# Adding the second part of half of the feed-forward weights by DMA, and three more pairs with seven block products

## The chip, the cores and the metric

The kernel runs on one core of one Trainium2 chip. The metric is device microseconds (us) of one execution. The median of three runs before the change is 1647.92 us (1647.09 to 1648.18).

## The reference, cut to what matters

A trunk of two layers works on 256 latent and 256 context tokens of width 1024. Each layer is a SwiGLU feed-forward block (FFN), a token mixer, and a second FFN:

```
D_MODEL = 1024; SEQ = CTX_LEN = 256; DEPTH = 2; D_FF = 2816

def swiglu(h, w_i, w_o):
    g, u = jnp.split(h @ w_i, 2, axis=-1)
    return (jax.nn.silu(g) * u) @ w_o

def trunk_layer(...):
    xl = xl + 0.5 * g1l * swiglu(modulate(rmsnorm(xl, norm_w[0]), sh1l, sc1l), w_ffn1_in, w_ffn1_out)
    xc = xc + 0.5 * g1c * swiglu(modulate(rmsnorm(xc, norm_w[0]), sh1c, sc1c), w_ffn1_in, w_ffn1_out)
    ...                      # the mixer: latent attention and a short convolution, then w_out
    xl = xl + 0.5 * g3l * swiglu(modulate(rmsnorm(xl, norm_w[2]), sh3l, sc3l), w_ffn2_in, w_ffn2_out)
    if not last:
        xc = ...             # the same for the context
```

Shifts, scales and gates come from `silu(c) @ w_ada[i] + b_ada[i]`. In the second layer the context stops after the mixer, so the last FFN has 256 tokens; the three FFNs before it have 512.

## The kernel before, in words

**Two parts of each number.** TensorE multiplies in its `float32r` type. Each operand is kept as two such tiles: the high part is the number cast to `float32r` (`whi`, `h`, `hid`), and the low part is the number minus the high part (`wlo` for weights). A product is three matmuls (`mm3`, L227 to L229): high by high, high by low, low by high. `split` makes the parts: ScalarE casts (L233), VectorE subtracts (L234).

**Weights.** `wload` (L206) loads a weight tile of 128x1024 (512 KB) into one of three `wraw` buffers by a DMA that SP issues, and splits it into one of five `whi` and one of five `wlo` buffers. Such a tile holds eight blocks of 128x128. Inside the mixer every fourth tile has its subtraction on GpSimd (L221).

**FFN, first product.** The 2816 hidden columns are 22 pairs of a gate block and an up block of 128 columns, 11 pairs in each of two halves. `gated` computes a pair plainly: two weight tiles, 2x8 blocks, three matmuls of 512 tokens each, 48 matmuls. `gated_fast` computes a pair with seven products of half-size matrices in place of eight (Winograd's form): 7 x 4 blocks x 3 matmuls of 256 tokens, 84 matmuls. It needs sums of weight blocks, made in place in `wraw` by four VectorE operations (L454 to L458), four split tiles (`wg`, `w22` of half size, `s12`, `s34`), and more VectorE operations on the results (L485 to L495). `FAST` lists the pairs done so: 6, 8 and 8 of 22 in the three FFNs of 512 tokens. The last FFN (`ffn_end`) has none.

**FFN, second product.** After each half, `into_x` multiplies 11 tiles of the output weights (`f1o`, `f2o`) with the hidden blocks: eight output blocks, each a sum of 11 blocks by three matmuls of 512 tokens, and adds them to X (L346). In the second half, the last three output blocks are done for the context first and then for the latents (`apart`), and the norm of the next part starts between them: squares on ScalarE, sums on VectorE and TensorE, a power -1/2 on GpSimd (`r`, L248), its broadcast on TensorE (`psn_r`, L251), then `t` (L301), `h` (L302) and the low part of `h` (L303).

**Modulation.** `ada` puts loads of `w_ada` (512 KB each) and two VectorE operations for each between the other work, at a rate set by `PACE`.

**Order.** The kernel is written in program order, and a scheduler arranges each engine's instructions by a model of time when it is built; `issue_after` holds some behind others. Each engine then works its own list in order. A DMA that waits holds whatever stands behind it on the engine that issues it: SP for the loads, GpSimd for the DMAs of the change.

Of the kernel before, what the change touches and what calls it, by code (L numbers as in the profile page):

```python
# [13 lines left out]
AF = mybir.ActivationFunctionType  # L14
ALU = mybir.AluOpType
# [5 lines left out]
NKT = D // P  # L21
# [18 lines left out]
WCH = 1024  # L40
# [15 lines left out]
LEAD = 1  # L56
EARLY_AT = (1, 1, 2, 2, 3, 3)
NT1 = 3
PACE = ((0.9, 2.15), (0.8, 1.7), (0.9, 1.75))
FAST = ((8, 10, 13, 15, 17, 19), (6, 8, 10, 12, 14, 16, 18, 20), (6, 8, 10, 12, 14, 16, 18, 20))  # L60


@with_exitstack
def tile_kernel(ctx: ExitStack, tc: tile.TileContext, xT, ctxT, cT, cR, w_ada, b_ada, norm_w,
                f1i, f1o, f2i, f2o, f2r, w_in, qn_w, kvn_w, w_uq, w_ukv, conv_w, w_out, fin_w,
                qtab, out):
    nc = tc.nc
# [137 lines left out]

    turn, pooled = [0], [False]  # L206

    def wload(src, n, tags=("whi", "wlo"), by=None):
        raw = slot("wraw", "wraw")[:, :n]
        load(raw, src)  # L210
        if by is not None:
            nc.vector.tensor_tensor(raw, raw, by, ALU.mult)
        w = [slot(t, "w" + p, dtype=F32R)[:, :n] for t, p in zip(tags, ("hi", "lo"))]
        turn[0] += 1
        if not (pooled[0] and turn[0] % POOLED == 0):
            split(*w, raw)
            return w
        nc.scalar.copy(w[0], raw)  # L218
        for a in range(0, n, TT):
            c = slice(a, a + TT)  # L220
            nc.gpsimd.tensor_tensor(w[1][:, c], raw[:, c], f32(w[0][:, c]), ALU.subtract)  # L221
        return w
# [9 lines left out]
    def split(hi, lo, src, eng=nc.vector):  # L232
        nc.scalar.copy(hi, src)  # L233
        return eng.tensor_tensor(lo, src, f32(hi), ALU.subtract)  # L234
# [19 lines left out]
    class Norm:  # L254
# [38 lines left out]
        def apply(self, s, R, kt):  # L293
# [5 lines left out]
            hi, lo = (h[:, cs] for h in self.H[kt])  # L299
            t1 = small.tile([P, T], F32, tag="t1", name="t1", bufs=NT1)  # L300
            nc.vector.scalar_tensor_tensor(t1, x, mod(d, 3 * i + 1, s, kt), R, ALU.mult, ALU.mult)  # L301
# [18 lines left out]
    def into_x(d, gate, streams, src, xs, nxt, pace=(0, 0)):  # L320


        n = len(xs)
        held = {}
        if nxt is not None and nxt.d < DEPTH and len(streams) == 1:
            ada_until(nxt.d, 3 * nxt.i + 1)

        def block(b):
            i = b // NKT
            if i not in held:  # L330
                held[i] = wload(src(i), WCH)
            return [v[:, b % NKT * P:(b % NKT + 1) * P] for v in held[i]]

        for ms in (range(0, NKT - SKEW), range(NKT - SKEW, NKT)):
            apart = nxt is not None and ms.stop == NKT
            if apart and nxt.d < DEPTH:
                ada_until(nxt.d, 3 * nxt.i + 1)
            for c in spans(streams, apart):
                for m in ms:
                    pt = mmtile(c)  # L340
                    for k in range(n):
                        mm3(pt, block(m * n + k), [v[:, c[0]:c[1]] for v in xs[k]], k == 0, k == n - 1)
                    for s in streams:
                        if c[0] <= s * T < c[1]:
                            xm = X[m][:, s * T:(s + 1) * T]
                            end = nc.vector.scalar_tensor_tensor(xm, pt[:, s * T - c[0]:(s + 1) * T - c[0]],  # L346
                                                                 mod(d, gate, s, m), xm, ALU.mult, ALU.add)
                            if nxt is not None:
                                nxt.add(m, s)
                                if nxt.d < DEPTH and len(streams) == 1:  # L350
                                    nxt.ahead(m, s)
                    if not apart:
                        ada(pace[1], end)
                if apart:
                    nxt.finish(c[0] // T)


    def gated(d, wi, j, nrm, streams):
# [1 line left out]
        H = nrm.H  # L360
        done = [early.pop(0) for _ in range(2)] if early else None
        if not done:
            w = [wload(wi[d, j, gu], WCH) for gu in range(2)]
        hid = pair(HID[j % HALF % 3], "hid")
        if nrm.AX and j < NAHEAD:

# [24 lines left out]
    def moving_sums(H):  # L391
# [44 lines left out]
            put(3, x)  # L436
        return out

    def gated_fast(d, wi, j, H, sums):

        g, u = (slot("wraw", "wraw") for _ in range(2))
        load(g, wi[d, j, 0])
        load(u, wi[d, j, 1])
        a, b = slice(0, TT), slice(TT, WCH)

        def parts(src):
            n = src.shape[-1]
            w = [slot(t, "w" + p, dtype=F32R)[:, :n] for t, p in (("whi", "hi"), ("wlo", "lo"))]
            split(*w, src)
            return w  # L450

        wg = parts(g)
        w22 = parts(u[:, b])
        nc.vector.tensor_tensor(g[:, a], g[:, a], u[:, a], ALU.subtract)  # L454
        nc.vector.tensor_tensor(u[:, a], u[:, a], u[:, b], ALU.add)
        nc.vector.tensor_tensor(u[:, b], u[:, b], g[:, a], ALU.subtract)
# [144 lines left out]
    def mixer(d, H, last, nxt):  # L601
# [15 lines left out]
        for c in spans([0, 1], True):  # L617
# [6 lines left out]
            product(ps, w[1], H, c)  # L624
            k1 = small.tile([P, T], F32, tag="t1", name="k1", bufs=NT1)
            k2 = small.tile([P, T], F32, tag="t1", name="k2", bufs=NT1)
            nc.vector.scalar_tensor_tensor(k1[64:96], ps[96:128], math.sqrt(QKD), qtb[96:128, cs], ALU.mult, ALU.mult)
# [145 lines left out]
        def attend(h, s, pT):  # L773
# [9 lines left out]
            r = slice(h % 2 * VD, (h % 2 + 1) * VD)  # L783
            o = small.tile([P, T], F32, tag="t1", name="o1", bufs=NT1)[r]
            nc.scalar.copy(o, ps[VD:P])
# [178 lines left out]
```

## Time and profile before

| | |
|---|---|
| median of three runs | 1647.92 us |
| the profiled execution | 1648.4 us, span 1646.6 us |
| TensorE (PE) busy | 1612.0 us, 98% |
| VectorE (DVE) busy | 1248.0 us, 76% |
| ScalarE (ACT) busy | 688.4 us, 42% |
| GpSimd (POOL) busy | 57.6 us, 3% |
| loads from SP's queue | 247.62 MB, 44.1% of 16 DMA engines |

The profile is of one execution. "Busy" is time in which an engine executed something; the DMA share is the mean over the core's 16 DMA engines. A row of a group gives line, engine, operation, output and inputs, shapes, count, then busy time and the mean of one in ns, then the idle time just before and who ended it. A row of the timeline gives start, duration, engine, line, operation, tile, shape and count. A matmul's recorded duration is its way through the array; the next one starts before it is over.

### The profile page before, as it was taken

What the parts mean: (1) busy time and instruction counts of PE and PEld (TensorE: products, weight loads), DVE (VectorE), ACT (ScalarE), POOL (GpSimd) and SP (SyncE); (2) the same over time, 40 slices, a digit from 0 to 9 for tenths busy, and PEclk for the clock granted to TensorE, in tenths of its full rate; (3) what the DMA queues carried; (4) which work ended last, traced back from release to release, by engine and by line L of the source; (5) the groups of instructions that cost most, each with busy time, mean ns of one, the idle gap of its engine ahead of it and who ended that gap; (6) DMA issues with size and microseconds to landing.
All of it is one profiled execution on the core that took longest, in us unless ns stands there. A gap on an engine that the chain in (4) does not pass through costs nothing.

```text
span 1646.6 us, 24595 instructions
## 1 busy us (share of the span) xinstructions
PE 1612.0 (98%) x9677; PEld 1415.4 (86%) x9677; DVE 1248.0 (76%) x2071; ACT 688.4 (42%) x1103; POOL 57.6 (3%) x65
## 2 busy tenths in 40 slices
PE   6999999999999999999999999999999999999998
PEld 5889889889877788988998888988998998989997
DVE  5597898888477578879887879876776578776665
ACT  4434224424476443431343243431443257754443
POOL 0000000001211000000000000000000011100000
PEclk9999999999999999999999999999999999999999
DMA  9434664562222124346444533365346333345553
GB/s 374 144 114 155 223 197 162 175 205 103 72 80 71 52 103 141 122 160 211 160 140 168 192 111 116 133 233 190 128 147 219 103 99 114 128 156 190 182 190 105
DMA packets 73364, 249.72 MB, mean 152 GB/s; under 512 B 8736, under 2 KB 12960, under 8 KB 73248
## 3 DMA queue, kind: packets, MB, share of 16 engines
q1 hardware_dynamic: 72960, 247.62, 44.1%
q8 instruction: 76, 1.25, 0.3%
q10 hardware_dynamic: 288, 0.52, 0.1%
q14 instruction: 40, 0.33, 0.1%
HBM read 246.28 MB, written 1.05 MB: 150 GB/s over the span
## 4 chain that ended last, share of the span: by engine, by line
PE 95%; DVE 2%; ACT 1%; issue 1%; DMA 1%; POOL 0%; SPq 0%; POOLq 0%; DVEq 0%
PE mm L227 25%; PE mm L228 25%; PE mm L229 25%; PE psg L229 2%; PE psg L228 2%; PE psg L227 2%; PE pso L780 1%; PE pse L227 1%; PE pse L228 1%; PE pse L229 1%; PE pst L767 1%; PE mme L227 1%; PE mme L229 1%; PE mme L228 1%; PE psn_s L243 1%
## 5 line engine op out<-in xcount | busy, mean ns | idle before, releaser
L233 ACT CAST whi<-wraw 128x1024 fp32r<-128x1024 f32 (+1 forms) x349 | 354.6, 1021 | 669.1 <-PE mm L228 418.3
L234 DVE TENSOR_TENSOR wlo<-wraw,whi 128x1024 fp32r<-128x1024 f32 (+1 forms) x349 | 414.3, 1191 | 135.5 <-ACT whi L233 129.4
L228 PE MATMUL mm<-h,whi 128*128 128x256 f32 (+1 forms) x1472 | 495.9, 338 | 3.9 <-DVE h L303 3.6
L227 PE MATMUL mm<-h,whi 128*128 128x256 f32 (+1 forms) x1472 | 496.0, 341 | 1.8 <-ACT h L302 1.3
L229 PE MATMUL mm<-h,wlo 128*128 128x256 f32 (+1 forms) x1472 | 494.3, 337 | 0.0
L227 PEld LDWEIGHTS mm<-h,whi 128*128 128x128 f32 x1472 | 277.8, 190 | 38.7 <-issue 7.3
L228 PEld LDWEIGHTS mm<-h,whi 128*128 128x128 f32 x1472 | 280.0, 190 | 33.7 <-DVE h L303 5.4
L229 PEld LDWEIGHTS mm<-h,wlo 128*128 128x128 f32 x1472 | 279.8, 190 | 28.9
L228 PE MATMUL mm<-hid,whi 128*128 128x512 f32 (+1 forms) x627 | 222.5, 356 | 0.0
L229 PE MATMUL mm<-hid,wlo 128*128 128x512 f32 (+1 forms) x627 | 222.4, 356 | 0.0
L227 PE MATMUL mm<-hid,whi 128*128 128x512 f32 (+1 forms) x627 | 221.9, 356 | 0.0
L174 DVE SCALAR_TENSOR_TENSOR wa<-wa,scb 128x1024 f32<-128x1024 f32 x128 | 155.2, 1217 | 0.6
L229 PEld LDWEIGHTS mm<-hid,wlo 128*128 128x128 f32 x627 | 118.5, 189 | 16.8
L227 PEld LDWEIGHTS mm<-hid,whi 128*128 128x128 f32 x627 | 118.5, 189 | 16.7
L228 PEld LDWEIGHTS mm<-hid,whi 128*128 128x128 f32 x627 | 118.5, 189 | 16.6
L174 DVE SCALAR_TENSOR_TENSOR junk<-wa,scb 128x1024 f32<-128x1024 f32 x96 | 117.5, 1224 | 9.0 <-DMA wa<-in_w_ada 8.0
L346 DVE SCALAR_TENSOR_TENSOR X<-mm,mod,X 128x256 f32<-128x256 f32 x120 | 53.5, 478 | 51.1 <-PE mm L229 50.9
L233 ACT CAST hid<-sg 128x512 fp32r<-128x512 f32 (+1 forms) x88 | 49.1, 560 | 36.7 <-DVE sg L495 20.4
L234 DVE TENSOR_TENSOR hid<-sg,hid 128x512 fp32r<-128x512 f32 (+1 forms) x88 | 53.9, 613 | 12.2 <-ACT hid L233 12.2
L221 POOL TENSOR_TENSOR wlo<-wraw,whi 128x512 fp32r<-128x512 f32 x18 | 24.6, 1388 | 787.4 <-ACT whi L218 787.4
L227 PE MATMUL mm<-ts,whi 128*128 128x256 f32 x176 | 49.8, 283 | 0.0
L228 PE MATMUL mm<-ts,whi 128*128 128x256 f32 x176 | 49.8, 283 | 0.0
(238 smaller groups left out, 2273.4 us busy)
## 6 DMA issues: line engine op xcount, KB each, us to landing
wa<-in_w_ada SPq DMA_DIRECT2D x128, 512.0 KB, 4.4
wraw<-in_f1i SPq DMA_DIRECT2D x88, 512.0 KB, 3.6
wraw<-in_f2i SPq DMA_DIRECT2D x88, 512.0 KB, 3.5
wraw<-in_f1o SPq DMA_DIRECT2D x44, 512.0 KB, 3.5
wraw<-in_w_in SPq DMA_DIRECT2D x32, 512.0 KB, 3.5
wraw<-in_f2o SPq DMA_DIRECT2D x22, 512.0 KB, 3.5
wraw<-in_f2r SPq DMA_DIRECT2D x22, 512.0 KB, 4.2
waf<-in_w_ada SPq DMA_DIRECT2D x16, 512.0 KB, 8.2
```

Of the source, the lines that this page charges most:

```text
L174: nc.vector.scalar_tensor_tensor(junk, wt, 1.0, scb[:, s, :], ALU.mult, ALU.mult, accum_out=md[:, s, ct:ct + 1])
L221: nc.gpsimd.tensor_tensor(w[1][:, c], raw[:, c], f32(w[0][:, c]), ALU.subtract)
L227: nc.tensor.matmul(ps, w[0], x[0], start=start, stop=False)
L228: nc.tensor.matmul(ps, w[0], x[1], start=False, stop=False)
L229: last_mm[0] = nc.tensor.matmul(ps, w[1], x[0], start=False, stop=stop)
L233: nc.scalar.copy(hi, src)
L234: return eng.tensor_tensor(lo, src, f32(hi), ALU.subtract)
L243: nc.tensor.matmul(ss[:, t:t + 1], sq[:, t * P:(t + 1) * P], mean_col[n_mean], start=(i == 0), stop=(i == len(sqs) - 1))
L346: end = nc.vector.scalar_tensor_tensor(xm, pt[:, s * T - c[0]:(s + 1) * T - c[0]], mod(d, gate, s, m), xm, ALU.mult, ALU.add)
L767: end = nc.tensor.transpose(pt[:, kt * P:(kt + 1) * P], pr[:, kt * P:(kt + 1) * P], ident)
L780: end = nc.tensor.matmul(ps[r0:r0 + VD, :], V[kt][:, h * VD:(h + 1) * VD], pT[:, kt, :], start=kt < 2, stop=kt >= nkt - 2, tile_position=( ...
```

## The change

Half of the FFN's input weight tiles in plain pairs (the gate block of each pair), all tiles of FFN output weights, and in the fast pairs `wg` and `w22`, get their low part by a new function, `lent`: ScalarE casts the raw tile to the high part, ScalarE writes minus that rounded tile into the low buffer (a copy with scale -1), and a DMA issued by GpSimd reads the raw weights from HBM a second time and adds them onto it in SBUF. VectorE no longer subtracts there. Mixer weights keep the old way. There are 176 such DMAs, 151 of 512 KB and 25 of 256 KB. `FAST` goes from 6, 8, 8 to 7, 9, 9 pairs.

```
+LENT = 2
+LEND = (1, 2, 1, 1)
-FAST = ((8, 10, 13, 15, 17, 19), (6, 8, 10, 12, 14, 16, 18, 20), (6, 8, 10, 12, 14, 16, 18, 20))
+FAST = ((8, 10, 12, 14, 16, 18, 20), (6, 8, 10, 11, 13, 15, 17, 19, 21), (6, 8, 10, 12, 13, 15, 17, 19, 21))
...
-    def wload(src, n, tags=("whi", "wlo"), by=None):
+    def wload(src, n, tags=("whi", "wlo"), by=None, lend=0):
...
         turn[0] += 1
+        if lend and turn[0] % LENT < lend:
+            lent(w, raw, src)
+            return w
         if not (pooled[0] and turn[0] % POOLED == 0):
             split(*w, raw)
             return w
...
-                held[i] = wload(src(i), WCH)
+                held[i] = wload(src(i), WCH, lend=LEND[1] if n > NKT else 0)
...
-            w = [wload(wi[d, j, gu], WCH) for gu in range(2)]
+            w = [wload(wi[d, j, gu], WCH, lend=LEND[0]) for gu in range(2)]
...
+    def lent(w, raw, src):
+
+        nc.scalar.copy(w[0], raw)
+        nc.scalar.activation(w[1], raw, AF.Copy, scale=-1.0)
+        nc.gpsimd.dma_start(w[1], src, accum_op=ALU.add)
...
-        def parts(src):
+        def parts(src, dram=None):
...
-            split(*w, src)
+            if dram is None:
+                split(*w, src)
+            else:
+                lent(w, src, dram)
             return w
 
-        wg = parts(g)
-        w22 = parts(u[:, b])
+        wg = parts(g, wi[d, j, 0] if LEND[2] else None)
+        w22 = parts(u[:, b], wi[d, j, 1, :, b] if LEND[3] else None)
```

How it moves instructions, at three places. First ScalarE in the first FFN's `into_x`, where six output-weight tiles are prepared one after the other (numbers tell buffers apart). Before, each takes one instruction:

```order
L233 CAST whi_1746<-wraw_1744 128x1024
L233 CAST whi_1776<-wraw_1774 128x1024
L233 CAST whi_1819<-wraw_1817 128x1024
L233 CAST whi_1866<-wraw_1864 128x1024
L233 CAST whi_1913<-wraw_1911 128x1024
```

Now, at the same place:

```order
L446 CAST whi_1763<-wraw_1761 128x1024
L447 ACTIVATE wlo_1764<-wraw_1761 128x1024
L446 CAST whi_1794<-wraw_1792 128x1024
L447 ACTIVATE wlo_1795<-wraw_1792 128x1024
L446 CAST whi_1838<-wraw_1836 128x1024
L447 ACTIVATE wlo_1839<-wraw_1836 128x1024
```

Each tile now has a second ScalarE instruction, which writes the `wlo` buffer that VectorE wrote before.

Second, VectorE at the norm after the second FFN (`v` is the norm's sum plus epsilon, `acc` a sum of squares, `t1` and `h` the normed tiles). Before:

```order
L234 TENSOR_TENSOR wlo_8887<-wraw_8884,whi_8886 128x1024
L283 TENSOR_TENSOR acc0_5638<-acc0_5638,sq_8680 128x256
L346 SCALAR_TENSOR_TENSOR X_109<-mm_8726,mod0_8_132,X_109 128x256
L234 TENSOR_TENSOR wlo_8893<-wraw_8890,whi_8892 128x1024
L283 TENSOR_TENSOR acc1_5639<-acc1_5639,sq_8761 128x256
L246 TENSOR_SCALAR v_8686<-psn_s_8683 128x2
L234 TENSOR_TENSOR wlo_9015<-wraw_9012,whi_9014 128x1024
L346 SCALAR_TENSOR_TENSOR X_109<-mm_8764,mod0_8_132,X_109 128x256
L301 SCALAR_TENSOR_TENSOR t1_8694<-X_109,mod1_1_134,psn_r_8690 128x256
L301 SCALAR_TENSOR_TENSOR t1_8698<-X_109,mod1_1_134,psn_r_8690 128x256
L301 SCALAR_TENSOR_TENSOR t1_8702<-X_109,mod1_1_134,psn_r_8690 128x256
L234 TENSOR_TENSOR wlo_9021<-wraw_9018,whi_9020 128x1024
```

Now:

```order
L239 TENSOR_TENSOR wlo_9113<-wraw_9110,whi_9112 128x1024
L288 TENSOR_TENSOR acc1_5746<-acc1_5746,sq_8980 128x256
L251 TENSOR_SCALAR v_8905<-psn_s_8902 128x2
L351 SCALAR_TENSOR_TENSOR X_109<-mm_8983,mod0_8_132,X_109 128x256
L288 TENSOR_TENSOR acc1_5746<-acc1_5746,sq_9018 128x256
L306 SCALAR_TENSOR_TENSOR t1_8913<-X_109,mod1_1_134,psn_r_8909 128x256
L306 SCALAR_TENSOR_TENSOR t1_8917<-X_109,mod1_1_134,psn_r_8909 128x256
L306 SCALAR_TENSOR_TENSOR t1_8921<-X_109,mod1_1_134,psn_r_8909 128x256
L239 TENSOR_TENSOR wlo_9242<-wraw_9239,whi_9241 128x1024
L308 SCALAR_TENSOR_TENSOR h_8912<-t1_8913,mod1_0_133,h_8912 128x256
```

Two of four weight subtractions in this stretch are gone; the last one, between `t1` and `h`, stays (the next tile's, further down, is gone).

Third, GpSimd's own list at that norm and its neighbours. Before, the powers stand one behind the other:

```order
L234 TENSOR_TENSOR mixa_5083<-o2_5157,mixa_5083 64x256
L248 TENSOR_TENSOR r_5471<-v_5469,mhalf_90 128x2
L248 TENSOR_TENSOR r_5601<-v_5599,mhalf_90 128x2
L248 TENSOR_TENSOR r_8688<-v_8686,mhalf_90 128x2
L248 TENSOR_TENSOR r_8845<-v_8843,mhalf_90 128x2
```

Now:

```order
L448 DMA wlo_8870<-in_f2o 128x1024
L448 DMA wlo_9106<-in_f1i 128x1024
L253 TENSOR_TENSOR r_8907<-v_8905,mhalf_90 128x2
L448 DMA wlo_9235<-in_f1i 128x1024
L448 DMA wlo_9309<-in_f1i 128x1024
L253 TENSOR_TENSOR r_9064<-v_9062,mhalf_90 128x2
L448 DMA wlo_9447<-in_f1i 128x1024
```

The DMAs of the change stand in front of, between and behind the two powers of the norm.

## The prediction

> **What bounds the kernel now.** I read the page first: busy times, the rows by time, the chain that ended last.
>
> ```profile
> span 1646.6 us, 24595 instructions
> PE 1612.0 (98%) x9677; PEld 1415.4 (86%) x9677; DVE 1248.0 (76%) x2071; ACT 688.4 (42%) x1103; POOL 57.6 (3%) x65
> ...
> GB/s 374 144 114 155 223 197 162 175 205 103 72 80 71 52 103 141 122 160 211 160 140 168 192 111 116 133 233 190 128 147 219 103 99 114 128 156 190 182 190 105
> ...
> PE 95%; DVE 2%; ACT 1%; issue 1%; DMA 1%; POOL 0%; SPq 0%; POOLq 0%; DVEq 0%
> ```
>
> TensorE bounds it: 95% of the chain, and 34.6 us of the span in which it does nothing. Next the waits of PE, longest first (who waited, for whom, us in total, times, longest):
>
> ```profile
> PE psn_s L243 <- DVE sums L843: 6.1, 4, 3.1
> PE psa L146 <- DMA waf<-in_w_ada: 5.3, 2, 5.2
> PE mm L228 <- DVE h L303: 3.6, 5, 1.7
> PE psn_r L251 <- POOL r L248: 2.6, 2, 2.3
> ...
> PE pst L767 <- ACT pr L754: 0.2, 1, 0.2
> ```
>
> These are 14 rows, 27.3 us together. The first two belong to the start of the program, the third to norms. None names a weight tile of an FFN: VectorE's subtractions, 76% busy or not, hold TensorE up nowhere inside the FFNs. So taking work off VectorE is worth nothing by itself there. What the change can earn must come from TensorE's own work or from the norms.
>
> **The change part by part.**
>
> *Three more fast pairs.* The timeline of PE around a fast pair gives the spacing of matmuls:
>
> ```profile
> 117.67 0.39 PE L227 MATMUL mm<-h,whi 128*128 128x512 f32 x1
> ...
> 124.47 0.28 PE L227 MATMUL mm<-h,whi 128*128 128x256 f32 x1
> ...
> 133.10 0.40 PE L227 MATMUL mm<-h,whi 128*128 128x512 f32 x1
> ```
>
> From 117.67 to 124.47 thirty matmuls of 512 columns start, 0.2267 us each; from 124.47 to 133.10 seventy-two of 256 columns, 0.1199 us each. A plain pair is 48 x 0.2267 = 10.88 us, a fast pair 84 x 0.1199 = 10.07 us. Seven products for eight would be an eighth, 1.36 us, but the half-width matmul costs more than half. Saved: 0.81 us a pair, **2.4 us** for three, all on the path.
>
> *VectorE and ScalarE.* The groups, with forms kept apart:
>
> ```profile
> L234 DVE TENSOR_TENSOR wlo<-wraw,whi 128x1024 fp32r<-128x1024 f32 x325 | 397.2, 1227 | 129.5 <-ACT whi L233 123.5 <-PE mm L229 4.3
> L233 ACT CAST whi<-wraw 128x1024 fp32r<-128x1024 f32 x325 | 339.7, 1050 | 614.8 <-PE mm L228 403.2 <-PE psg L228 62.1 <-issue 59.3
> L234 DVE TENSOR_TENSOR wlo<-wraw,whi 128x512 fp32r<-128x512 f32 x24 | 17.1, 711 | 6.0 <-ACT whi L233 6.0
> L454 DVE TENSOR_TENSOR wraw<-wraw 128x512 f32<-128x512 f32 x22 | 15.0, 683 | 0.0
> ```
>
> The 151 big and 25 small lent tiles take 151 x 1.23 + 25 x 0.71 = 203 us off VectorE; a fast pair costs it about eight half-size operations and one more big subtraction than a plain pair, some 6 us, 18 for three. It falls to about 1063 us. ScalarE gets 151 x 1.05 + 25 x 0.62 = 174 us (the nearest row for the copy with scale is the cast) and reaches about 860 us, 52%. Neither is the bound, so this term is 0; its cover is the 615 us that ScalarE idles before its casts, mostly for a `whi` buffer that PE still reads. The new copy waits for a `wlo` buffer instead, freed one matmul later (0.23 us); behind it on ScalarE stand the squares, `sg` and `h`, for which TensorE waits only at the norms.
>
> *The way of a lent tile.* How long it may take is seen on ScalarE's casts in an `into_x` stretch:
>
> ```profile
> 182.81 1.06 ACT L233 CAST whi<-wraw 128x1024 fp32r<-128x1024 f32 x1 [4.39 <-PE mm L228]
> 188.25 1.05 ACT L233 CAST whi<-wraw 128x1024 fp32r<-128x1024 f32 x1 [4.38 <-PE mm L228]
> ```
>
> One tile is eaten in 24 x 0.2267 = 5.44 us, the distance of these casts. A cast fills the buffer just freed, and with five buffers its tile is needed four tiles later, 21.8 us on. The two ScalarE passes take 2.1 us of that. The trace before has no DMA that adds, and none that GpSimd issues. The nearest rows:
>
> ```profile
> wraw<-in_f1o SPq DMA_DIRECT2D x44, 512.0 KB, 3.5
> waf<-in_w_ada SPq DMA_DIRECT2D x16, 512.0 KB, 8.2
> L221 POOL TENSOR_TENSOR wlo<-wraw,whi 128x512 fp32r<-128x512 f32 x18 | 24.6, 1388 | 787.4 <-ACT whi L218 787.4
> ```
>
> A plain load of the same size lands in 3.5 us, the loads crowded together at the start in 8.2. I take 5, above the plain load because of the added read. That leaves 21.8 - 2.1 - 5 = **14.7 us** of cover in `into_x`. Where a plain and a fast pair alternate, six tiles go in 20.95 us and four tiles are 14 us: 6.9 us of cover. By latency alone nothing stalls, term 0.
>
> *The DMA engines.* By rate it is closer. Windows (columns: stretch, length, busy time and count of PE, PEld, DVE, ACT, POOL, then clock, DMA share and GB/s) of `into_x` in the first FFN, of its alternating pairs, of `into_x` in the third FFN, and of the last FFN:
>
> ```profile
> 160.00:225.00 65.00, 65.00 (x291) 53.91 (x291) 56.88 (x91) 14.71 (x16) 0.00 (x0) 1.00 0.61 203
> 240.00:330.00 90.00, 90.00 (x546) 80.83 (x545) 77.03 (x115) 37.02 (x49) 0.00 (x0) 1.00 0.49 170
> 1080.00:1140.00 60.00, 60.00 (x275) 50.01 (x275) 41.35 (x66) 13.26 (x14) 0.00 (x0) 1.00 0.67 231
> 1460.00:1600.00 140.00, 137.78 (x975) 129.54 (x974) 93.92 (x114) 65.37 (x92) 0.00 (x0) 1.00 0.54 178
> ```
>
> In `into_x` a lent tile adds 0.524 MB every 5.44 us, 96 GB/s. At the plain rate (0.61 for 203 GB/s) that is a share of 0.29. Call r the cost of a lent byte in plain bytes. It can't be under 1, since the same bytes are read from HBM again. An upper end: the destination is read too and then written, at most three passes, r = 3. The share is 0.61 + 0.29r: 0.90 at r = 1, 1.48 at r = 3. Between, I take r = 1.5 for the sum, nearest the plain load, which is the only row of this size: 1.05, a backlog of 0.05 x 60 = 3 us at the end of a half (11 tiles, 60 us), far under the cover. The alternating pairs add 2.5 tiles in 20.95 us, 62 GB/s, so 0.49 + 0.18r, below 1 up to r = 2.8; the last FFN adds about as much to 0.54, below 1 up to 2.5. Term 0, as long as 0.61 + 0.29r stays under 1 + 14.7/60: r up to 2.2, or 2.0 in the third FFN (0.67).
>
> The Trainium skill has a rule for this price: in "Collectives: The Full Stack", Part 3 (why ReduceScatter is half of AllGather), an add in the DMA engines needs two source reads and so delivers half the rate of a copy. No run before shows it; by it r would be 2 and the sum would be the one of the second rival below.
>
> *Norms.* The chain at the norm after the second FFN, on VectorE:
>
> ```profile
> 958.10 1.26 DVE L301 SCALAR_TENSOR_TENSOR t<-X,mod,psn_r 128x256 f32<-128x256 f32 x3 [0.74 <-PE psn_r L251]
> 959.28 1.22 DVE L234 TENSOR_TENSOR wlo<-wraw,whi 128x1024 fp32r<-128x1024 f32 x1
> 960.75 1.27 DVE L303 SCALAR_TENSOR_TENSOR h<-t,mod,h 128x256 fp32r<-128x256 f32 x3
> 962.72 1.22 DVE L234 TENSOR_TENSOR wlo<-wraw,whi 128x1024 fp32r<-128x1024 f32 x1
> ```
>
> Two weight subtractions stand inside the norm's own work. In the new order the one at 959.28 stays and the one at 962.72 goes, but a tile's cast and copy stand between `h` on ScalarE where one cast stood. So up to 1.2 us is gained and up to 1.05 lost. The norms into the mixer are followed by mixer weights, which are not lent. With two norms into FFNs of 512 or 256 tokens after a mixer and this one, bounds are -3.6 and +3.1 us; I take 0.
>
> *GpSimd's queue.* The powers of the norm now have DMAs in front. What covers them:
>
> ```profile
> 593.60 0.70 POOL L248 TENSOR_TENSOR r<-v,mhalf 128x2 f32<-128x2 f32 x1 [23.42 <-DVE v L246]
> 596.74 0.60 PE L251 MATMUL psn_r<-ident,r 128*128 128x128 f32 x4
> 966.78 0.70 POOL L248 TENSOR_TENSOR r<-v,mhalf 128x2 f32<-128x2 f32 x1 [11.58 <-DVE v L246]
> 967.81 0.60 PE L251 MATMUL psn_r<-ident,r 128*128 128x128 f32 x4
> ```
>
> The first power ends 2.4 us before TensorE gets to its broadcast, the second only 0.3 us. What GpSimd needs to issue an adding DMA no row shows. It could be nothing that holds the power up; I bound it above by GpSimd's 1.39 us for half a tile (above). A power caught behind one loses up to 1.1 us at such a second norm; the pair of matmul groups already running there is the next cover. Three norms: 0 to 3.3 us; I take 0, since two DMAs of one list rarely fall just there.
>
> **Sum.** -2.4 us and zeros. The profiled execution took 1648.4 us, 0.5 over the median of the runs; so 1646.0 against it and **1645.5 us** against the median. This is -0.15%; 0.2%, 3.3 us, is about what a measurement here can tell from none.
>
> **The rivals.**
>
> *The norms gain.* Three subtractions fewer on the chains, -3.6 us more at best, half of it likely: 1642 to 1644.6. For it: the chain rows above. Against: ScalarE's new copies stand on the same chain.
>
> *The transfers cost twice (r = 2), or GpSimd's powers come late.* Slower by a little. In `into_x` shares of 1.19 (four halves) and 1.25 (two), backlogs of 11 and 15 us. They fit just into 14.7 us. If a lent DMA takes 10 us rather than 5, cover is 9.7, and TensorE waits 1.7 x 4 + 5.3 x 2 = 17 us. So 1646 to 1663 us, with 1650 in the middle; the late powers alone give up to 1649. For it: two reads for one write, loads on the same 16 engines, and 374 GB/s as the fastest slice of the page (the GB/s row above), where 203 + 192 would be wanted. This is what the skill's rule makes of the time.
>
> *The transfers cost 2.5 to 3 times.* Shares of 1.34 and 1.40 at 2.5: backlogs of 20 and 24 us, 5.5 x 4 + 9.3 x 2 = 41 us lost, 1686; at 3, 1.48 and 1.54, (28.8 - 14.7) x 4 + (32.4 - 14.7) x 2 = 92 us, 1737. In the trace PE would wait for `wlo` again and again in `into_x`, with the load queue of SP late too. It decides from r = 2.2. Nothing in the profile speaks for a rate so low, and nothing excludes it.
>
> **How the numbers follow.** Hidden, with only the pairs' gain: 0.32, of it 0.24 within 0.2% and 0.08 beyond (1644 to 1647 is its own range). Norms gain as well: 0.22, all faster. Twice the cost or late powers: 0.28, of it 0.06 within 0.2%, 0.22 slower. 2.5 times and more: 0.18, slower. That makes faster 0.30, same 0.30, slower 0.40, with the first the likeliest single case. The range runs from 1642 (the better half of the norms' gain left out) to 1685 (r = 2.5), leaving out about 0.03 below and 0.1 above.
>
> **What would show it.** Right: 252 matmuls of 256 columns in place of 144 of 512, PE busy down by about 2.4 us, VectorE near 1063 and ScalarE near 860 us; lent DMAs landing in about 5 us; no row of PE waiting for a DMA into `wlo`. Wrong: rows of PE `mm` L234 waiting for that DMA, above all in `into_x` late in a half with the DMA share there at 0.95 or more; a DMA that lands later than 15 us; `psn_r` waiting for `r` behind GpSimd's DMAs. If PE busy falls by 2.4 and the span by far more, the norms did it.

## The result and the profile after

The changed kernel takes 1731.77 us (median; 1728.07 to 1740.43) against 1647.51 us: 1.0519 times the time before, with a 95% interval of 1.048 to 1.0559. Forecast were 1645.5 us and a range up to 1685. The profiled execution took 1728.07 us, with a span of 1726.3 us, 79.7 us longer than before. Its page: span, busy times, the two DMA queues (packets, MB, share of the 16 engines' time), and the chain that ended last.

```profile
span 1726.3 us, 25372 instructions
PE 1637.4 (95%) x9785; PEld 1432.5 (83%) x9785; DVE 1092.2 (63%) x1929; ACT 845.3 (49%) x1288; POOL 208.6 (12%) x239
...
q1 hardware_dynamic: 72960, 247.62, 41.9%
q0 software_dynamic: 25344, 85.73, 26.5%
...
PE 54%; issue 17%; DMA 17%; DVE 7%; ACT 3%; POOL 2%; SPq 0%; POOLq 0%; DVEq 0%; ACTq 0%
```

TensorE's share of the chain falls from 95 to 54%; DMA, which had 1%, has 17%. The queue rows give the price of a lent byte. The loads of SyncE (q1) move 247.62 MB in 41.9% of the engines' time, 342 GB/s; the adding DMAs (q0) move 85.73 MB in 26.5%, 187 GB/s. So r = **1.83** plain bytes, under the 2.2 from which the forecast saw a loss. VectorE has 156 us less to do than before, ScalarE 157 us more.

TensorE's waits (who, for whom, us in total, times, longest); the trace of before had 27.3 us together and no tile `wlo` among them:

```profile
PE mm L234 <- DMA wlo<-in_f2i: 18.8, 16, 3.4
PE mm L234 <- DMA wlo<-in_f2o: 6.2, 3, 4.3
PE mm L234 <- DMA wlo<-in_f1i: 6.1, 7, 1.4
...
PE mm L232 <- ACT hid L238: 4.5, 2, 3.7
...
PE psn_r L256 <- POOL r L253: 2.3, 1, 2.3
PE mm L234 <- DMA wlo<-in_f1o: 1.7, 2, 1.1
```

All 23 rows sum to 81.1 us, 54 more than before. The lent tiles' own are 32.8 us; the rest is new lateness of other things. The mean granted clock of TensorE falls from 0.997 to 0.985, which is up to 21 us more lost to half speed (0.015 of 1726.3 us against 0.003 of 1646.6). The landings (KB each, median us from issue):

```profile
wa<-in_w_ada SPq DMA_DIRECT2D x128, 512.0 KB, 7.1
...
wraw<-in_f1o SPq DMA_DIRECT2D x44, 512.0 KB, 7.9
...
wlo<-in_f2i POOLq DMA_DIRECT2D x44, 512.0 KB, 8.3
...
wlo<-in_f2o POOLq DMA_DIRECT2D x22, 512.0 KB, 9.7
```

A lent tile lands in 8.3 to 9.7 us, not in 5; and loads of others are late with it: those of `f1o` take 7.9 us where they took 3.5, the tiles of `w_ada` 7.1 (4.4 in the kernel before). The windows of `into_x` in the first FFN, its alternating pairs, `into_x` in the third FFN and part of the last FFN (columns as in the prediction; DMA share and GB/s last):

```profile
160.00:225.00 65.00, 65.00 (x288) 53.89 (x287) 37.09 (x67) 20.73 (x23) 8.71 (x10) 1.00 0.95 270
240.00:330.00 90.00, 82.34 (x464) 71.22 (x464) 64.05 (x107) 39.61 (x51) 9.58 (x11) 0.93 0.74 207
1130.00:1190.00 60.00, 59.21 (x267) 48.94 (x267) 27.15 (x49) 22.05 (x24) 9.54 (x11) 1.00 1.05 313
1520.00:1660.00 140.00, 129.60 (x884) 119.72 (x883) 67.88 (x87) 73.01 (x101) 12.21 (x14) 0.98 0.81 215
```

In `into_x` the share is 0.95 and 1.05 (it adds up the packets' times, so it can pass 1): the engines are full. In the pairs and in the last FFN they are not (0.74, 0.81), and yet TensorE idles there, 7.7 of 90 us and 10.4 of 140.

Two stretches show how that comes about. The first is the end of the first `into_x`: the list of SyncE, then what VectorE, ScalarE and TensorE waited for (start, length, engine; in brackets the idle time before and its releaser).

```profile
215.39 15.73 SPq L102 DMA_DIRECT2D wa<-in_w_ada  x5
231.93 0.33 SPq L102 DMA_DIRECT2D wraw<-in_f1i  x1
...
242.16 1.23 DVE L176 SCALAR_TENSOR_TENSOR junk<-wa,scb 128x1024 f32<-128x1024 f32 x1 [3.81 <-DMA wa<-in_w_ada]
...
244.03 0.62 ACT L238 CAST hid<-sg 128x512 fp32r<-128x512 f32 x1 [12.94 <-DVE sg L390]
244.55 1.04 ACT L238 CAST whi<-wraw 128x1024 fp32r<-128x1024 f32 x1
...
245.65 0.80 PE L232 MATMUL mm<-h,whi 128*128 128x512 f32 x1 [3.52 <-ACT whi L238]
```

VectorE's waits for `w_ada` tiles are 19.9 us from 155 to 217 us (the first `into_x`), and 8.0 us in the whole of the kernel before. SyncE issues its loads in order. From 215.4 to 231.1 it gets out five loads of `w_ada`, one by one, as VectorE frees their buffers; VectorE, behind after its waits, is busy for 14.3 of the 16.2 us up to 231.2. So the next weight load goes out only at 231.93, and the next `w_ada` tile at 234.34. They land 8.9 and 7.8 us later, at 240.8 and 242.1. VectorE waits 3.81 us for the second. Its `sg` stands behind that tile, ScalarE's cast of `hid` waits for `sg`, and the cast of the weight tile stands behind `hid`: it starts at 244.55, 3.7 us after its own load landed. At 245.65 TensorE has waited 3.52 us for that high part. The wait names neither the lent tile nor the DMA.

The second is the last FFN, where the lent tiles are waited for directly. The waits of TensorE for them and of VectorE for `f2r` in its stretch (1510 us to the end), one case on ScalarE, GpSimd and TensorE, and the three windows of TensorE's work at half clock there (columns as above):

```profile
PE mm L234 <- DMA wlo<-in_f2i: 16.2, 14, 3.4
DVE wraw L214 <- DMA wraw<-in_f2r: 76.4, 20, 9.1
```

```profile
1565.43 1.05 ACT L446 CAST whi<-wraw 128x1024 fp32r<-128x1024 f32 x1 [2.99 <-PE mm L233]
1568.11 0.89 POOL L448 DMA_DIRECT2D wlo<-in_f2i  x1 [12.81 <-PE mm L554]
1576.52 0.38 PE L234 MATMUL mm<-h,wlo 128*128 128x256 f32 x1 [0.88 <-DMA wlo<-in_f2i]
```

```profile
1508.38:1515.21 6.83, 4.67 (x21) 4.67 (x22) 1.23 (x1) 0.70 (x1) 0.90 (x1) 0.50 0.97 257
1542.51:1545.93 3.42, 3.42 (x18) 3.42 (x18) 2.26 (x2) 1.04 (x1) 0.00 (x0) 0.50 0.77 242
1597.13:1600.54 3.41, 3.41 (x16) 3.31 (x16) 2.78 (x3) 0.67 (x1) 0.00 (x0) 0.50 0.98 246
```

The `whi` buffer comes free at 1565.43; cast, minus-copy and `sg` take until 1567.7, the issue follows, and TensorE wants the tile at 1575.64, 10.2 us after the cast's start. The tile lands some 8.4 us after the issue, and TensorE waits 0.88 us. The row of waits has 14 such cases. In the windows TensorE works 11.5 us at half clock, which costs about 5.8 us more (an estimate from these rows). Together that is 22.0 us; the last FFN takes 22.2 us longer than before (the table of stages below).

### The profile page after: what moved, and what is told of

It reads as the page before. It is cut to its first block, busy times and chain, and to the rows that moved or that the text cites. A ratio compares the mean times of both kernels' runs of the same rounds, so it can differ in the third digit from the quotient of the medians.

```text
span 1726.3 us, 25372 instructions
## 1 busy us (share of the span) xinstructions
PE 1637.4 (95%) x9785; PEld 1432.5 (83%) x9785; DVE 1092.2 (63%) x1929; ACT 845.3 (49%) x1288; POOL 208.6 (12%) x239
## 3 DMA queue, kind: packets, MB, share of 16 engines
q1 hardware_dynamic: 72960, 247.62, 41.9%
q0 software_dynamic: 25344, 85.73, 26.5%
HBM read 332.00 MB, written 1.05 MB: 193 GB/s over the span
## 4 chain that ended last, share of the span: by engine, by line
PE 54%; issue 17%; DMA 17%; DVE 7%; ACT 3%; POOL 2%; SPq 0%; POOLq 0%; DVEq 0%; ACTq 0%
PE mm L234 14%; PE mm L232 14%; PE mm L233 14%; DMA wlo<-in_f2i 5%; DMA wa<-in_w_ada 5%; DMA wraw<-in_f1o 2%; POOL wlo L448 2%; DMA wlo<-in_f1i 1%; PE pso L794 1%; DVE junk L176 1%; DVE wa L176 1%; DMA wlo<-in_f2o 1%; DVE wlo L239 1%; PE pst L781 1%; ACT wlo L447 1%
## 5 line engine op out<-in xcount | busy, mean ns | idle before, releaser
L234 PE MATMUL mm<-h,wlo 128*128 128x256 f32 (+1 forms) x1448 | 487.5, 339 | 26.1 <-DMA wlo<-in_f2i 15.4
L232 PE MATMUL mm<-h,whi 128*128 128x256 f32 (+1 forms) x1448 | 487.9, 342 | 9.1 <-ACT h L307 4.4
L233 PE MATMUL mm<-h,whi 128*128 128x256 f32 (+1 forms) x1448 | 487.0, 338 | 1.3 <-DVE h L308 1.3
L238 ACT CAST whi<-wraw 128x1024 fp32r<-128x1024 f32 x180 | 187.4, 1044 | 302.6 <-PE mm L233 129.9
L234 PEld LDWEIGHTS mm<-h,wlo 128*128 128x128 f32 x1448 | 277.9, 192 | 62.0 <-DMA wlo<-in_f2i 20.5
L446 ACT CAST whi<-wraw 128x1024 fp32r<-128x1024 f32 (+1 forms) x176 | 173.8, 988 | 277.4 <-PE mm L233 101.5
L239 DVE TENSOR_TENSOR wlo<-wraw,whi 128x1024 fp32r<-128x1024 f32 x180 | 221.3, 1231 | 74.9 <-ACT whi L238 65.5
L234 PE MATMUL mm<-hid,wlo 128*128 128x512 f32 (+1 forms) x627 | 226.1, 361 | 8.0 <-DMA wlo<-in_f2o 6.2
L232 PE MATMUL mm<-hid,whi 128*128 128x512 f32 (+1 forms) x627 | 224.8, 360 | 4.5 <-ACT hid L238 4.5
L233 PE MATMUL mm<-hid,whi 128*128 128x512 f32 (+1 forms) x627 | 225.3, 359 | 0.0
L447 ACT ACTIVATE wlo<-wraw 128x1024 fp32r<-128x1024 f32 (+1 forms) x176 | 174.8, 993 | 6.0 <-PE pse L233 6.0
L176 DVE SCALAR_TENSOR_TENSOR junk<-wa,scb 128x1024 f32<-128x1024 f32 x96 | 117.8, 1227 | 80.4 <-DMA wa<-in_w_ada 79.7
L234 PEld LDWEIGHTS mm<-hid,wlo 128*128 128x128 f32 x627 | 120.5, 192 | 26.3 <-DMA wlo<-in_f2o 7.3
L448 POOL DMA_DIRECT2D wlo<-in_f1i x57 | 49.8, 874 | 444.2 <-ACT wlo L447 407.7
L448 POOL DMA_DIRECT2D wlo<-in_f2i x53 | 46.3, 874 | 413.4 <-ACT wlo L447 298.0
L214 DVE TENSOR_TENSOR wraw<-wraw,gb 128x1024 f32<-128x1024 f32 x22 | 26.9, 1225 | 77.7 <-DMA wraw<-in_f2r 77.7
```

The lines of the kernel that those rows point to most:

```text
L176: nc.vector.scalar_tensor_tensor(junk, wt, 1.0, scb[:, s, :], ALU.mult, ALU.mult, accum_out=md[:, s, ct:ct + 1])
L232: nc.tensor.matmul(ps, w[0], x[0], start=start, stop=False)
L233: nc.tensor.matmul(ps, w[0], x[1], start=False, stop=False)
L234: last_mm[0] = nc.tensor.matmul(ps, w[1], x[0], start=False, stop=stop)
L447: nc.scalar.activation(w[1], raw, AF.Copy, scale=-1.0)
L448: nc.gpsimd.dma_start(w[1], src, accum_op=ALU.add)
```

## The experiments

The letters in the expectations: A, an adding DMA takes more of the engines' time and so transfers land late; B, ScalarE's new passes; C, the new pairs and their order; D, the way over GpSimd and its DMAs' own latency; E, in the later ones, an adding DMA is late by itself, however full the engines.

### One part of the change alone

The new pairs, nothing lent:

```
-LEND = (1, 2, 1, 1)
+LEND = (0, 0, 0, 0)
```

> The changed kernel with no tile lent (LEND all 0), so VectorE subtracts everywhere as before; only the three more seven-product pairs are left. Theory A (the adding transfers load the DMA engines and delay every load) expects the pairs' own saving, 3 x 0.81 = 2.4 us: 1645 us, ratio 0.9985, PE without waits for weights. Rival C (the new pairs and the order they bring cost the time) expects it near the changed kernel, over 1700 us.

Measured: 1656.43 us, 1.0052 [1.0039, 1.0064]. Slower by 8.7 us: neither the 2.4 us gain nor a large loss. Two of its waits on TensorE that were shorter before (2.6 us for `r`, 1.3 for `h`):

```profile
PE psn_r L256 <- POOL r L253: 5.8, 3, 3.2
...
PE mm L232 <- ACT h L307: 4.8, 5, 2.1
```

The pairs' own 0.8 us each is there (the table below), but norms come late. That VectorE's added work ahead of them has no room is what the run without the DMA bears out, below, where VectorE is relieved. The other part, the lending with the old pairs:

```
-FAST = ((8, 10, 12, 14, 16, 18, 20), ...)
+FAST = ((8, 10, 13, 15, 17, 19), ...)      # the table of the kernel before
```

> The changed kernel with the old list of pairs (6, 8, 8), so lending alone. Theory A: 1732 + 2.4 = 1734 us, within 10 us. Rival C: near 1648 us.

Measured: 1724.87 us (one run), 77 us slower. The lending carries the loss.

### What of the lending: ScalarE, latency or rate

ScalarE's copies as in the changed kernel, without the DMA:

```
-        nc.gpsimd.dma_start(w[1], src, accum_op=ALU.add)
```

> The changed kernel without the adding DMA: ScalarE still casts and copies each lent tile, nothing is transferred a second time (the output leaves the sum out, the low part is minus the weights). Theory A: all of the loss goes, 1643 to 1646 us. Rival B (ScalarE's second pass on an engine that works in order delays casts, squares and h): most of the loss stays, over 1690 us.

Measured: 1644.63 us, 0.9982 [0.9973, 0.9991]. Neither ScalarE's 175 us nor the order costs anything; with VectorE relieved the pairs' gain appears, -3 us. B falls. The same DMA, copying instead of adding:

```
-        nc.gpsimd.dma_start(w[1], src, accum_op=ALU.add)
+        nc.gpsimd.dma_start(w[1], src)
```

> The changed kernel, same order of instructions on every engine, with the lent DMA a plain copy in place of an add (the output leaves the sum out). In the profile of the changed kernel an added byte took 1.8 times the DMA engine time of a loaded byte. Theory A, rate: at 1 instead of 1.8 the loads land in 4 to 5 us again and three quarters of the loss goes, 1650 to 1670 us. Rival D (the lent DMA's fixed latency, GpSimd's issue and landing, against the cover of five buffers): a copy has the same issue and nearly the same landing, so most of the loss stays, over 1700 us.

Measured: 1651.13 us, 1.0029 [1.0017, 1.0042]. Its queues, landings and first `into_x`:

```profile
q1 hardware_dynamic: 72960, 247.62, 43.8%
q0 software_dynamic: 25344, 85.73, 15.4%
...
wlo<-in_f1o POOLq DMA_DIRECT2D x44, 512.0 KB, 6.6
wlo<-in_f2i POOLq DMA_DIRECT2D x44, 512.0 KB, 5.7
```

```profile
160.00:225.00 65.00, 65.00 (x289) 53.81 (x288) 45.59 (x81) 21.40 (x23) 4.96 (x10) 1.00 0.79 266
```

The same bytes, issues and order: the copy's bytes cost the engines what plain ones do (r = 1.0), the share in `into_x` is 0.79, and of the 84 us only 3.6 are left. So 80.6 us hang on add against copy, and the way over GpSimd as such (D) falls.

Whether the adding DMA's length in itself or the DMA's being one that adds does it, half-length adds tell:

```
-        nc.gpsimd.dma_start(w[1], src, accum_op=ALU.add)
+        q = raw.shape[-1] // 2
+        nc.gpsimd.dma_start(w[1][:, :q], src[:, :q], accum_op=ALU.add)
```

> Every lent tile is made as in the changed kernel, but the adding DMA brings only the first half of its columns (42.9 MB added instead of 85.7); the other half of the low part stays minus the high part, so the sums leave it out. Theory A (engine time): at 1.83 plain bytes for an added byte the 42.9 MB cost the engines what 78 MB of plain loads would, less than the 85.7 MB of plain copies that came out at 1651.1 us; so 1643 to 1655 us, and the waits of L234 for the adding DMA as good as gone. Theory E (an adding DMA is late by itself, however full the engines are): the DMAs are half as long, but each still reads, adds and writes; half of the 84 us stays, 1680 to 1700 us.

Measured: 1660.99 us, 1.0074 [1.0048, 1.01]. Between, much nearer to A: 13.5 us left of 84, not 42. Its queues:

```profile
q1 hardware_dynamic: 72960, 247.62, 44.8%
q0 software_dynamic: 25344, 42.87, 15.4%
```

That is the same share of the engines as the copies of the run before (15.4%), for half the bytes: per byte these shorter adds cost even 2.0. A's sum had put them at 1.83 and so a little too low. As many adding DMAs as in the changed kernel, at the engine time of copies, cost 10 us more than copies.

### The price by itself

The kernel before, with a tail behind its output in which nothing else uses the DMA engines (shortened):

```
+        for n in (WCH, TT):                       # 512 KB, 256 KB; all into one tile, one after the other
+            for k in range(4): nc.sync.dma_start(m[:, :n], f1i[0, k, 0, :, :n])
+            for k in range(4): nc.gpsimd.dma_start(m[:, :n], f1i[0, k, 0, :, :n])
+            for k in range(4): nc.gpsimd.dma_start(m[:, :n], f1i[0, k, 0, :, :n], accum_op=ALU.add)
...                                                # then 12 of each kind into three tiles in turn
```

> The kernel before with a tail behind its output, when nothing else uses the DMA engines: loads of 512 KB and of 256 KB one after the other into one tile, plain by SyncE, plain by GpSimd, adding by GpSimd (four each), and then twelve of 512 KB of each kind into three tiles in turn. It measures the disputed price by itself. Theory A (an adding DMA costs 1.83 plain bytes of the engines, and the 8 to 10 us of its landing in the changed kernel are mostly queueing behind other transfers): alone, the adding one of 512 KB lands about 1.3 us after the copying one, at 4.5 to 5.5 us. Theory E (it is late by itself): 7 us or more alone.

Measured (one run, 1819.63 us with the tail). Issues of GpSimd, a copying (L616) and an adding (L618) one; then the median landings of four of each, and windows of the crowded part, twelve copies and twelve adds with three in flight:

```profile
1663.26 0.56 POOL L616 DMA_DIRECT2D wraw<-in_f1i  x1 [3.53 <-DMA wraw<-in_f1i]
...
1680.84 0.90 POOL L618 DMA_DIRECT2D wraw<-in_f1i  x1 [4.96 <-DMA wraw<-in_f1i]
```

```profile
wraw<-in_f1i POOLq DMA_DIRECT2D x4, 512.0 KB, 3.6
```

```profile
wraw<-in_f1i POOLq DMA_DIRECT2D x4, 512.0 KB, 5.5
```

```profile
1760.00:1780.00 20.00, 0.00 (x0) 0.00 (x0) 0.00 (x0) 0.00 (x0) 5.96 (x11) 0.50 0.87 298
1784.00:1809.00 25.00, 0.00 (x0) 0.00 (x0) 0.00 (x0) 0.00 (x0) 7.59 (x9) 0.50 1.03 196
```

Alone, a copy of 512 KB lands in 3.6 us, an add in 5.5: A's upper end, not E's 7 or more. Three adds at a time fill the engines (share 1.03) at 196 GB/s, and their landing rises to a median of 7.5 us. The forecast's 5 us was near what an add takes alone. In the changed kernel it is never alone.

### Where: output weights, gate and up tiles, plain pairs

```
+LEND = (0, 2, 0, 0)      # output weights only, all in into_x: 66 DMAs, 34.6 MB
```

> Only the output weights' tiles are lent (66 adding DMAs, 34.6 MB, all in into_x); gate and up tiles are split by VectorE as before, the pairs are the new ones. If into_x is where the engines fill up (share 0.95 there in the changed kernel) and the rest is its wake: 1685 to 1715 us. If each adding DMA is late on its own account, wherever it stands: 66 of 176 of the loss over the pairs alone, 1656 + 28 = 1684 us or less. If the pairs' own tiles make the loss (into_x had 14.7 us of cover): 1650 to 1665 us.

```
+LEND = (1, 0, 1, 1)      # gate and up tiles only: 110 DMAs, 51.1 MB
```

> The complement: gate and up tiles are lent (110 adding DMAs, 51.1 MB), the output weights' are not. If into_x makes the loss: 1645 to 1665 us, since the share of the engines stays under 0.75 in the pairs. If each adding DMA is late on its own account: 1656 + 52 = 1700 us or so. If the pairs' own tiles make the loss (cover of 6.9 us against landings over 8): 1700 to 1730 us.

Measured: 1696.55 us, 1.0315 [1.0284, 1.0346], and 1691.87 us, 1.0279 [1.0248, 1.0311]. Over the pairs alone (1656.43) that is 40.1 and 35.4 us, together 75.5; the changed kernel has 75.3. The two losses add up: `into_x` is not what makes the pairs slow, and neither place is free. The waits for lent tiles, first with the output weights alone, then with the rest alone:

```profile
PE mm L234 <- DMA wlo<-in_f2o: 5.2, 3, 3.0
...
PE mm L234 <- DMA wlo<-in_f1o: 4.5, 4, 1.9
```

```profile
PE mm L234 <- DMA wlo<-in_f2i: 19.0, 15, 3.4
...
PE mm L234 <- DMA wlo<-in_f1i: 2.5, 3, 1.1
```

In the pairs 21.5 us of 35.4 are direct waits for the lent tile; in `into_x` only 9.7 of 40.1. Lending in the plain pairs alone (60 DMAs of 512 KB):

```
+LEND = (1, 0, 0, 0)
```

> Lending in the plain pairs alone: 60 adding DMAs of 512 KB (31.5 MB of the 51.1 MB that the gate and up tiles had, which cost 35.5 us over the pairs alone). By bytes: 1656 + 22 = 1678 us. If the fast pairs carry the loss (three block sums and four tiles in 20 us): 1656 to 1665 us. If the plain pairs do (their tiles come in 10.9 us, with a cover of 6.9 us): 1685 us or more.

Measured: 1680.25 us, 1.0198 [1.0177, 1.022]: 23.8 us over the pairs alone, as by bytes, with 24.6 us in the rows of L234 waiting for lent tiles. Of the loss 17.0 us lie in the last FFN, and 15.1 us of the waits.

The stages, cut at the first and last matmul on `hid` of each `into_x` in the timeline of PE, and for the last FFN at its first matmul on `ax`, the operand of its first pairs (us before, then differences in the profiled executions; the stages left out differ by 2.3 us at most; the last column is the output weights alone with half the bytes of `w_ada`, below):

| stage | before | changed | pairs alone | copies | outputs only | gate, up only | outputs, half w_ada |
|---|---|---|---|---|---|---|---|
| first FFN, second half's pairs | 116.8 | +18.6 | -2.3 | +7.4 | +6.1 | +9.1 | +1.8 |
| first FFN, second into_x | 61.9 | +5.8 | +1.0 | 0.0 | +7.6 | +1.0 | +2.3 |
| mixer, then first half's pairs | 327.6 | +4.1 | +4.2 | -0.2 | -2.9 | +2.2 | +0.1 |
| second FFN, second half's pairs | 116.1 | +6.4 | -2.3 | -2.2 | +2.1 | +2.2 | +1.6 |
| second FFN, second into_x | 61.9 | +8.8 | +1.1 | +1.5 | +9.0 | +1.5 | +9.2 |
| third FFN, first half's pairs | 120.0 | +2.0 | +4.5 | -1.3 | +4.0 | +2.8 | +0.2 |
| third FFN, first into_x | 61.1 | +1.1 | 0.0 | 0.0 | +7.0 | 0.0 | +1.4 |
| third FFN, second into_x | 61.9 | +8.5 | +1.5 | +1.5 | +9.6 | +1.5 | +3.3 |
| mixer of the second layer | 125.4 | +1.6 | +1.6 | +1.6 | +1.7 | +1.9 | +4.4 |
| last FFN | 194.5 | +22.2 | 0.0 | +0.2 | 0.0 | +23.2 | 0.0 |

The largest losses stand where tiles were lent (last FFN with gate and up tiles, `into_x` with output weights) or, in the first FFN's second half, right behind a full stretch.

### Direct waits or crowding

Half of the bytes of `w_ada`, everything lent:

```
-        load(wt, w_ada[d, m, ct])
+        load(wt[:, :TT], w_ada[d, m, ct, :, :TT])      # VectorE reads these 512 columns twice
```

> The changed kernel with half of the w_ada loads' bytes: each of the 128 loads brings 512 of its 1024 columns, which VectorE uses twice (the modulations are therefore other numbers); VectorE's work stays the same size. That takes 33.6 MB of plain loads away and no adding DMA. Theory A (engine time; the weight loads are late because they share the engines with everything and stand behind the w_ada loads on SP's list): the surcharge of the 85.7 added MB is 0.83 of them, 71 MB, and this takes back nearly half of it, in just the stretches where the w_ada loads crowd; a time of 1660 to 1695 us. Theory E (only the lent tile's own DMA is late): the rows of L234 keep their 32.8 us and the time stays at 1720 us or more.

Measured: 1707.95 us, 1.0371 [1.035, 1.0393]: 23.8 us back, less than A's half and more than E allows. The waits for lent tiles hardly change: 29.0 us against 32.8. The same in the version with the output weights alone:

```
+LEND = (0, 2, 0, 0)      # and w_ada as above
```

> The version with the output weights alone lent (1696.6 us), with half of the w_ada loads' bytes as in the run on these. If what the lent tiles cost in into_x is that they hold up the w_ada tiles, behind which VectorE's norm work waits: 1660 to 1678 us. If it is the lent tile's own wait and what follows from it: 1688 us or more.

Measured: 1676.48 us, 1.0175 [1.0155, 1.0195]: 20.1 of the 40.1 us that the output weights' lending costs. Half of the loss is thus likely no matter of the lent tiles' own length, and hardly of waits for them: these are 8.9 us where they were 9.7. No run has half these bytes and nothing lent, so what the smaller loads give by themselves is not shown; with the pairs alone VectorE waits only 6.9 us for them. Its waits for `w_ada` are still 73.2 us here (78.0 with all the bytes), so whether it is the engines' time or the place in SyncE's list that these bytes take is not told apart.

Then more time ahead for each lent tile, at the same bytes. First the order on ScalarE together with the buffers:

```
-BUFS = {..., "whi": 5, "wlo": 5}
+BUFS = {..., "whi": 4, "wlo": 6}
...
-        nc.scalar.copy(w[0], raw)
         nc.scalar.activation(w[1], raw, AF.Copy, scale=-1.0)
         nc.gpsimd.dma_start(w[1], src, accum_op=ALU.add)
+        nc.scalar.copy(w[0], raw)
```

> The changed kernel with more time ahead for each adding DMA and not a byte less: ScalarE makes the minus-copy before the high part instead of behind it (0.99 us earlier), and there are six buffers for low parts and four for high parts instead of five and five. If the waits for the lent tiles themselves are the loss: the 32.8 us in L234's rows mostly go and the time falls to 1660 to 1695 us. If the engines' crowding is the loss, in whatever transfer it shows: the same bytes crowd as before, weight tiles, w_ada tiles and rows of f2r are as late as they were, and the time stays at 1710 us or more.

Measured: 1752.87 us, 1.0644 [1.062, 1.0668]. Slower by 21 us, the rows of L234 for lent tiles at 40.1 us. No clean test: a high buffer less may cost by itself. So the order alone, with five and five:

> The changed kernel with one difference: ScalarE makes the minus-copy, and GpSimd issues the adding DMA, ahead of the high part instead of behind it, at five and five buffers. Each adding DMA may start some 1 us earlier, each high part is 1 us later; bytes and counts are the same. If PE's waits for the lent tiles are most of the loss: 1700 us or less, L234's rows for them down from 32.8 us by a third or more. If crowding is (every other transfer stays as late): within 8 us of 1731.8.

Measured: 1731.47 us, 1.0521 [1.0492, 1.055], the changed kernel's time to 0.3 us. The waits:

```profile
PE mm L234 <- DMA wlo<-in_f2i: 18.9, 16, 4.3
...
PE mm L234 <- DMA wlo<-in_f1o: 5.7, 3, 3.3
...
PE mm L234 <- DMA wlo<-in_f2o: 4.4, 2, 2.9
...
PE mm L234 <- DMA wlo<-in_f1i: 3.8, 5, 1.0
```

32.8 us again, to the tenth. An instruction's length more ahead of the DMA buys nothing, even where the wait is direct. The high parts come as much later, though, and TensorE's rows for ScalarE's `hid` and `whi` (L238) go from 8.0 to 13.5 us, so this is no test of more time for free. The engine time that the DMAs take fits better as what sets the loss, and thinning them agrees, 18 output tiles instead of 66:

```
+LENT = 4
+LEND = (0, 1, 0, 0)
```

> The output weights' tiles lent by turns of four instead of all: 18 adding DMAs of 512 KB instead of 66, every second or fourth tile in into_x, none elsewhere. If each costs its share whatever its neighbours (40 us for 66 tiles over the pairs alone): 1656 + 11 = 1667 us. If the cost is crowding, which a transfer of 2.6 us in 11 to 22 us doesn't make: 1650 to 1658 us, no worse than the pairs without lending, and better by what VectorE saves ahead of the norm.

Measured: 1658.28 us, 1.006 [1.0048, 1.0073]. 1.9 us over the pairs alone, at the upper end of what was expected of crowding, and far from the 11 us of a price per tile: these 18 land no sooner (8.4 to 8.6 us), but no row of TensorE waits for one. A tile that lands late once in a while stays within its cover; tile after tile, with the others' loads late too, does not.

### The pairs at another place

```
-FAST = ((8, 10, 12, 14, 16, 18, 20), (6, 8, 10, 11, 13, 15, 17, 19, 21), (6, 8, 10, 12, 13, 15, 17, 19, 21))
+FAST = ((8, 10, 12, 13, 15, 17, 19), (6, 8, 10, 11, 12, 14, 16, 18, 20), (6, 8, 10, 11, 12, 14, 16, 18, 20))
```

> No lending; the three more pairs stand earlier in their half of the FFN (12 and 13 in the first, 11 and 12 in the other two), so that each half's last pairs are those of the kernel before. If the pairs alone cost 8.7 us because their VectorE work falls on the last pairs ahead of into_x and its norm: the loss goes, 1643 to 1650 us, down to the 2.4 us that the table of products gives. If VectorE lacks the time wherever they stand: 1652 to 1660 us.

Measured: 1654.48 us, 1.0047 [1.0034, 1.006]. The loss moves from the norms into the half where the pairs stand side by side (+5.8 us in the first FFN's second half) and stays. VectorE has no room for three more fast pairs in either place. No version with the reference's full sum beats the kernel before; the 1644.63 us without the DMA is what a free second part would give.

## Why the prediction was wrong, step by step

**Three more fast pairs: -2.4 us.** The matmuls came as said (108 more, 36 a pair), and in the second halves of the FFNs the pairs alone are 2.3 us shorter, of which `into_x` gives 1.0 to 1.5 back. Right in size. Where nothing else is in the way (no DMA) the sum is -3 us.

**VectorE and ScalarE: 0.** VectorE fell by 156 us (forecast 185), ScalarE rose by 157 (174): 0 for ScalarE is right. But "taking work off VectorE is worth nothing by itself" did not hold beside the new pairs: without the relief the pairs cost 8.7 us instead of saving 2.4, with it and without the DMAs they save 3. Relief was worth 11.8 us (1656.43 against 1644.63), as cover for the three pairs that the forecast had costed at 18 us of VectorE and then at nothing. What relief is worth with the old pairs no run shows.

**The way of a lent tile: 0 by latency.** This is the step that failed first. The landing was taken as 5 us; alone it is 5.5, in the kernel 8.3 to 9.7. Even so `into_x` kept cover for the lent tile itself: in the first `into_x` TensorE doesn't wait once, in all six 7.9 us for lent tiles. The cover of 6.9 us was worked out for pairs of 512 tokens only. The last FFN has 256, a pair every 194.5/22 = 8.8 us with three tiles, so four tiles are 11.8 us and, after ScalarE's 2.1 and a landing of 5, 4.7 us are left; with 8.3 us it is 1.4 on average. In the case shown, TensorE wants the tile after 10.2 us instead of 11.8, and nothing is left. There, 16.2 us of direct waits, with the half clock behind some of them, make the 22.2 us of loss.

**The DMA engines: 0 up to r = 2.2.** r was taken as 1.5 and is 1.83, which is still under the threshold; it is the threshold that failed. It let a backlog stand against the lent tile's cover alone, as if only lent tiles waited in it. The runs showed who else does: the tiles of `w_ada`, whose lateness holds VectorE, the casts of ScalarE that wait for VectorE's results (3.52 us for TensorE in the stretch above) and, in SyncE's ordered list, the weight loads (15.73 us in the same stretch); and the tiles of `f2r`, for which VectorE waits 77.7 us where it waited 25.0 before and 47.3 with the pairs alone. Half of the bytes of `w_ada` gave 20 us of 40 back.

The Trainium skill's rule for collectives, "Collectives: The Full Stack", Part 3 (why ReduceScatter is half of AllGather), that an add needs two source reads and so runs at half the rate of a copy, is near what the traces show: 1.83 in the kernel, and 1.8 alone by share and GB/s (0.87 for 298 against 1.03 for 196).

**Rivals.** The second (r = 2) had the mechanism and nearly the rate, with a lent DMA at 10 us, and priced it at 17 us where 84 came: it counted waits for lent tiles in `into_x` only, 60 us a half, and neither the pairs nor the last FFN nor the other loads. The third (2.5 to 3 times) had times near the measured one for a rate that isn't there.

**Norms and GpSimd's queue: 0 and 0.** The row of `psn_r` waiting for `r` is 2.3 us (2.6 before): right. Norms were no gain of their own with the adding DMAs; with the pairs alone they were a loss.

**What would show it.** "Rows of PE `mm` L234 waiting for that DMA" came, but not "above all in `into_x`": 16.2 of 32.8 us lie in the last FFN. The share of 0.95 or more in `into_x` came as named.

**What stays open.** The waits' 54 us more, up to 21 of the clock and the pairs' -2.4 account for at most 72 of the 79.7 us; the rest no row names. In the last FFN the account closes; over the whole kernel, how the loss divides between direct waits (32.8 us and the half clock behind them) and crowding is only bounded, and the engines' time was not told apart from SyncE's order, which wasn't tried in another order.

## What to carry to other kernels

When work moves to the DMA engines, price it as engine time in each stretch (an adding DMA at nearly two plain bytes) and then ask for every load in that stretch, not just the new one, who waits for it and what is queued behind it; a share of 0.6 before plus 0.35 is full. Work out the cover for the shortest stage as well, with the landing under load, which here is 1.5 to 1.8 times the landing alone. And relief of an engine that holds up nothing can still be the price of the other half of the change: cost both halves apart.

## What the runs showed of the hardware

TensorE's granted clock fell to half after waits. Between the start and the end of the program, the changed kernel has 11 stretches at half clock, 47.8 us together; the kernel before has one, of 6.8 us. Nine of the 11 last 3.41 us. In the changed kernel's timeline TensorE stands still ten times for 2 us or more behind the start; for nine of these gaps, the shortest of 2.05 us, half clock begins within 4.4 us of their start; for one (2.94 us, at 823.92) it does not. Windows behind the gaps of 2.18 us at 235.08 and 3.20 us at 409.02, and between them one at full clock:

```profile
238.60:242.00 3.40, 3.40 (x16) 2.81 (x14) 0.00 (x0) 0.00 (x0) 0.00 (x0) 0.50 1.04 389
...
256.00:266.00 10.00, 10.00 (x59) 8.83 (x58) 5.17 (x9) 4.04 (x5) 0.00 (x0) 1.00 0.47 141
412.80:416.20 3.40, 3.40 (x18) 3.40 (x17) 3.40 (x7) 0.42 (x1) 0.06 (x1) 0.51 0.62 169
```

A stretch of 3.41 us full of work costs 1.7 us more (an estimate: half of it). And an adding DMA takes GpSimd 0.87 us to issue, a copying one of the same shape 0.55 us.
